# A streaming encoder step on one core: small matmuls of the mixers given out at every second step, squares of the first sub-layer taken later and added on DVE

## The chip, the cores and the metric

The kernel runs on one core of one Trainium2 chip. The metric is device time in microseconds (us) of one execution; lower is better. The kernel before has a median of 1207.81 us over three runs (1206.51 to 1208.27). Times inside an execution come from one profiled run. The engines are named as in the profile: PE (TensorE, with PEld for its weight loads), DVE (VectorE), ACT (ScalarE), POOL (GpSimd) and SP (SyncE, which issues DMAs).

## The reference

The trunk has two layers. Each layer has three sub-layers with a norm in front and a norm behind: a half-step SwiGLU, a mixer, and another SwiGLU. All of it is fp32. 304 tokens are worked on at once: 16 meta tokens, 256 prompt frames and 32 frames of a running stream. The model width is 1024, the hidden width of the SwiGLU 2816.

```python
def half_ffn(x, g_pre, w_in, w_out, g_post):
    gate, up = jnp.split(rmsnorm(x, g_pre) @ w_in, 2, axis=-1)
    return x + 0.5 * rmsnorm((jax.nn.silu(gate) * up) @ w_out, g_post)
# mixer: z = pre_mix(x) @ w_in; z -> attn q,k,v | ret q,k,v | ret gate
p = exp(s - m) / (sum(exp(s - m)) + exp(sink - m))        # chunk-banded attention with a sink
scores = einsum('bnihd,bnjhd->bnhij', rot(q), rot(k)) * intra_decay   # retention
o = scores @ v + q_decay * (rot(q) @ state)
ret = o * rsqrt(mean(o * o) + EPS) * silu(gate)           # norm over each head, then the gate
x = x + rmsnorm(concat(attn, ret) @ w_out)
```

Per layer and mixer there are 8 attention heads in 2 groups and 8 retention heads in 4 pairs. Besides the final norm's result, the kernel writes the attention caches and the retention states.

## The kernel before, in words

Activations lie transposed, features on the 128 partitions and tokens along the free axis, so a product is a matmul of a 128x128 weight block with 128x304 activations. An fp32 product is made of three matmuls of a reduced type (`mm3`): high part of the weight by high part of the activation (L257), low by high (L258), high by low (L260). These are called large matmuls here; nearly all of PE's work is of them. Weights come from DRAM as raw tiles (SP's queue, L187 and L191) and are split just ahead of use: ACT copies the high part (L205), DVE subtracts to get the low part (L208).

A `group4` keeps four PSUM banks open and works through eight weight pieces of 12 large matmuls each, a `group2` keeps two open, with 6 large matmuls between its calls of `tick`. Nothing in the program waits by itself: the order in which instructions are written is the order in each engine's queue, and `tick(ns)` sets it. It advances a clock that stands for PE's time (775 for 6 large matmuls, 1550 for 12), splits the next weights, runs the jobs in `later` that are due, and then takes jobs from two threads: "a" (attention) and "r" (retention). Of each thread it takes one due job per call, and goes on only past a job marked as free. `flush` empties everything that is left.

A mixer (`mixer`, L765) begins with a `group4` for attention k, v and the first half of q, then nine `group2` (L1197 to L1207): the second half of q, then twice retention k, q and v, then the gate in two halves. What becomes ready is queued with due times:

- Attention, per unit of two chunks (`queue_attn`, L1148): scores (L1060), softmax on DVE and ACT (L1029, L1031, L1034, then L1038 to L1046), transposes of the probabilities (L1074) copied by ACT (L1083) and DVE (L1081), and their product with v (L1092). Units of the running stream and of the meta tokens have lines 1115, 1125 and 1139 for the same steps.
- Retention, per pair of heads p (`queue_ret`, L924): transposes of v (L887), scores (L900) multiplied by the decay on DVE (L905), output (L915 to L921) copied by ACT (L922), its square on ACT (`norm_sq`, L947), the norm's matmul (L952) with square root on ACT (L954), reciprocal on DVE (L955) and multiply on POOL (L956), and transposes of k (L845). Before that, rotated q and k are made: DVE multiplies as soon as a `group2` ends (L821, L822), SP moves rows (L825), POOL adds a `ROT` later (L828).

Behind the gate's two groups comes `flush` (L1208) and `gate_out`: silu on ACT (L1179), multiply on DVE (L1180), and the split of the product into high (L1182, ACT) and low (L1184, DVE). The output projection follows: its first four pieces are attention's, the other four the retention's.

The first sub-layer of the program has no sub-layer ahead of it, so `pre_norm` puts its work into `later` (L472 to L478): `prep(k)` makes the high half of activation k on ACT (L424) and the low half on DVE (L427); `stat_sq(k)` squares on ACT (L432) and adds on POOL (L434). Two buffers, tag "sq", hold squares. After the first `group4`, `stats` sums over the partitions with a matmul of ones (L483), and a square root (L486) and a reciprocal (L491) follow.

Of the kernel before, what the change touches and what calls it, by code (L numbers as in the profile page):

```python
# [17 lines left out]
KD = DM // P  # L18
# [25 lines left out]
X2 = 1000  # L44
TAILF = 4
CAP0 = 14
SQ0 = 500
SQD = 500
PREP = 800
KA = 6  # L50
START = (11000, 11713)
# [55 lines left out]
def tile_hybrid_step(ctx, tc, I, O):  # L107
    nc = tc.nc
    PE, ACT, DVE, POOL, SP = nc.tensor, nc.scalar, nc.vector, nc.gpsimd, nc.sync
# [7 lines left out]
    def bank():  # L117
        return ps.tile([P, 512], F32, tag="bk", name="bk")
# [48 lines left out]
    xw = []  # L167
# [7 lines left out]
        xw.pop().close()  # L175

    raws, split = {}, {}
    st = {"dma": 0, "split": 0, "use": 0, "free": 0, "xw": None, "cap": 1 << 30, "ramp": 0}

    def load_to(c, between=lambda: None):  # L180
        while st["dma"] < min(c, len(chunks)):
# [13 lines left out]
    def split_one():  # L195
        i = st["split"]
        eng = ACT if i else DVE
        load_to(i // 2 + 1)
        r = raws[i // 2][:, (i % 2) * 512:(i % 2) * 512 + 512]
        if i in extra:  # L200
            hi, lo = (st["xw"].tile([P, 512], F32R, name=f"{nm}{(i - 132) % 8}") for nm in ("xhi", "xlo"))
        else:
            hi, lo = (wp.tile([P, 512], F32R, tag=nm, bufs=BUFS, name=nm) for nm in ("hi", "lo"))
        if eng is ACT:
            ACT.activation(out=hi, in_=r, func=ACTF.Copy)  # L205
        else:
            eng.tensor_copy(hi, r)
        DVE.tensor_tensor(out=lo, in0=r, in1=hi.bitcast(F32), op=ALU.subtract)  # L208
        split[i] = (hi, lo)
        if i % 2:  # L210
            raws.pop(i // 2)
        st["split"] += 1
        load_to((i + 1) // 2 + RAWS)

    def advance(most=2):
        while most and st["split"] < min(st["cap"], 2 * len(chunks)) and ring[st["split"] + 1] - ring[st["free"]] <= AHEAD and (
                st["split"] not in extra or st["xw"]):
            split_one()
            most -= 1
# [9 lines left out]
    clock = [0.0]  # L229
    later = []  # L230
    A, R = threads["a"], threads["r"]

    def tick(ns):
        clock[0] += ns
        advance()
        while later and later[0][0] <= clock[0]:
            later.pop(0)[1]()
        for nm, q in threads.items():
            while q and clock[0] >= q[0][1]:
                f, _, free = q.pop(0)  # L240
                f()
                if not free:
                    break
# [18 lines left out]
    def group4(nk, xh, xl, n, order, done, tail=2, lead=1):  # L262
        bk = [bank() for _ in range(4)]
        ws = [piece() for _ in range(lead)]
        for part in range(2):
            for k in range(lead):
                for m in range(4):
                    mm3(bk[m][:, :n], ws[k], m, xh(k), xl(k), k == 0, False, (part,))
                st["free"] += part
                if lead > 1 or part:  # L270
                    tick(1550 if lead == 1 else 1033 - 516 * part)
        for k in range(lead, nk - tail):
            w = piece()
            for m in range(4):
                mm3(bk[m][:, :n], w, m, xh(k), xl(k), False, False)
            st["free"] += 1
            tick(1550)
        ws = [piece() for _ in range(tail)]
        st["last"] = ws[-1][0], xh(nk - 1), n
        for i, m in enumerate(order):  # L280
            for j in range(tail):
                k = nk - tail + j
                mm3(bk[m][:, :n], ws[j], m, xh(k), xl(k), k == 0, k == nk - 1)
            done(m, bk)
            if i == 3:
                st["free"] += tail
            tick(388 * tail)
        return bk
# [59 lines left out]
    def x_in(hf, w=(0, 0, 0)):  # L348
        for t, (t0, tn) in enumerate(TT):
            b = xb[3 * hf + t]  # L350
            if (hf, t) == (0, 2):
                PE.transpose(out=b[:, 64:80], in_=gr, identity=ident[0:16, 0:16])
            for k in range(4):
                PE.transpose(out=b[:, k * P:k * P + tn], in_=xtok[t][0:tn, (4 * hf + k) * P:(4 * hf + k + 1) * P],
                             identity=ident[0:tn, 0:tn])
            warm(w[t])
            src = b.rearrange("p (k t) -> p k t", k=4)[:, :, 0:tn]
            dst = x[:, 4 * hf:4 * hf + 4, t0:t0 + tn]
            if t == 1:
                ACT.activation(out=dst, in_=src, func=ACTF.Copy)  # L360
            else:
                if (hf, t) == (0, 2):
                    DVE.tensor_copy(gcol[:, 0:16], b[:, 64:80])
                DVE.tensor_copy(dst, src)
# [55 lines left out]
    def acts(n, dt=F32R):  # L420
        return [ap.tile([P, N], dt, tag="act", bufs=2 * KD, name="act") for _ in range(n)]

    def act_hi(k, ua, pre):
        ACT.activation(out=ua[k][:, T0:], in_=x[:, k, T0:], func=ACTF.Copy, scale=gain(*pre, k))  # L424

    def act_lo(k, ua, pre):
        DVE.scalar_tensor_tensor(out=ua[KD + k][:, T0:], in0=x[:, k, T0:], scalar=gain(*pre, k),  # L427
                                 in1=ua[k][:, T0:].bitcast(F32), op0=ALU.mult, op1=ALU.subtract)

    def stat_sq(k, acc, first, eng=POOL):  # L430
        sq = acc if k == first else ap.tile([P, N], F32, tag="sq", bufs=2, name="sq")
        ACT.activation(out=sq[:, T0:], in_=x[:, k, T0:], func=ACTF.Square)  # L432
        if k != first:
            eng.tensor_tensor(out=acc[:, T0:], in0=acc[:, T0:], in1=sq[:, T0:], op=ALU.add)  # L434

    def small(name, tag=None, bufs=1):
        return ap.tile([P, N], F32, tag=tag or name, bufs=bufs, name=name)

    def pre_norm(pre, prev):

        ua = acts(2 * KD)
        acc = small("acc")
        rb = small("rb")
        if prev:
            lo0 = prev.first(ua)
            for k in range(1, KD + 1):
                if k < KD:
                    prev.step(k)
                    act_hi(k, ua, pre)
                if k == 1:  # L450
                    lo0()
                if k > 2:
                    act_lo(k - 1, ua, pre)
                if k < 2:
                    act_lo(k, ua, pre)
                if k > 1:
                    stat_sq(k - 1, acc, 1, DVE if k > KA else POOL)
            prev.residual0()
            stat_sq(0, acc, 1, DVE)
        else:  # L460
            for k in range(4):
                act_hi(k, ua, pre)
                split_one()
                act_lo(k, ua, pre)

            def rest():
                x_in(1)
                start.close()

            def prep(k):  # L470
                act_hi(k, ua, pre)
                act_lo(k, ua, pre)  # L472
            later.append((X2, rest))
            for k in range(4, KD):
                later.append((X2 + PREP * (k - 3), lambda k=k: prep(k)))
            for k in range(KD):
                later.append((X2 + SQ0 + SQD * k, lambda k=k: stat_sq(k, acc, 0)))
            later.sort(key=lambda e: e[0])  # L478
        st["cap"] = st["use"] + (11 if prev else CAP0)

        def stats():
            b = bank()
            PE.matmul(out=b[:, T0:N], lhsT=ones, rhs=acc[:, T0:], start=True, stop=True)  # L483
            sd = small("sd")
            if prev is None:
                ACT.activation(out=sd[:, T0:], in_=b[:, T0:N], func=ACTF.Sqrt, scale=1.0 / DM, bias=epst)  # L486
            else:
                DVE.scalar_tensor_tensor(out=sd[:, T0:], in0=b[:, T0:N], scalar=1.0 / DM, in1=prev.se[:, T0:], op0=ALU.mult,
                                         op1=ALU.add)
                ACT.activation(out=sd[:, T0:], in_=sd[:, T0:], func=ACTF.Sqrt)  # L490
            DVE.reciprocal(out=rb[:, T0:], in_=sd[:, T0:])  # L491
            st["cap"] = 1 << 30

        return (lambda k: ua[k][:, T0:]), (lambda k: ua[KD + k][:, T0:]), rb, stats
# [85 lines left out]
    def ffn(pre, post, nxt, prev, after=None):  # L580
        last = nxt is None
        xh, xl, rb, stats = pre_norm(pre, prev)
        if after:
            after()
# [180 lines left out]
    def mixer(l, prev):  # L765
        nonlocal T0
        lastl = l == DEPTH - 1
        t0 = NMETA if lastl else 0
        xh, xl, rb, stats = pre_norm((2, l), prev)
        mix = ExitStack()  # L770
        mp = mix.enter_context(tc.tile_pool(name="mix", bufs=1, reuse_waits="tile"))
# [490 lines left out]
```

## Time and profile before

| what | kernel before |
|---|---|
| median of three runs | 1207.81 us (1206.51 to 1208.27) |
| profiled execution: its own time | 1207.66 us |
| profiled execution: span of the trace | 1205.9 us |
| mean granted clock of PE | 0.994 of full |
| PE busy, instructions | 1181.7 us, 8746 |
| DVE busy, instructions | 833.0 us, 1503 |
| ACT busy, instructions | 589.6 us, 1208 |
| POOL busy, instructions | 184.2 us, 198 |

Busy time is the time in which an engine had an instruction of its own running; overlapping matmuls count once. The page of the profile gives it for the span, and again in 40 slices. For a kernel that is bound by one engine, the share says little on what a change is worth; the timeline (each instruction with its start and length), the waits (what an engine stood still for) and the chain of waits (followed back from the last instruction) say more. In the timeline, neighbours of one form on one engine are folded into one row with a count (x2), whose length is from the start of the first to the end of the last. Two engines' rows are interleaved by start. A bracket at the end gives the idle time of the engine just before and what ended it.

### The profile page before, as it was taken

What the parts mean: (1) busy time and instruction counts of PE and PEld (TensorE: products, weight loads), DVE (VectorE), ACT (ScalarE), POOL (GpSimd) and SP (SyncE); (2) the same over time, 40 slices, a digit from 0 to 9 for tenths busy, and PEclk for the clock granted to TensorE, in tenths of its full rate; (3) what the DMA queues carried; (4) which work ended last, traced back from release to release, by engine and by line L of the source; (5) the groups of instructions that cost most, each with busy time, mean ns of one, the idle gap of its engine ahead of it and who ended that gap; (6) DMA issues with size and microseconds to landing.
All of it is one profiled execution on the core that took longest, in us unless ns stands there. A gap on an engine that the chain in (4) does not pass through costs nothing. (4 is left out here: it accounts for less than half of the span.)

```text
span 1205.9 us, 22846 instructions
## 1 busy us (share of the span) xinstructions
PE 1181.7 (98%) x8746; PEld 1147.7 (95%) x8746; DVE 833.0 (69%) x1503; ACT 589.6 (49%) x1208; POOL 184.2 (15%) x198
## 2 busy tenths in 40 slices
PE   8999999999999999999999999999999999999996
PEld 8999999998899999999989999999988999999996
DVE  6766664587888766675586665747778988666543
ACT  6644444455455545444454444445554655454441
POOL 4200001130143200022030000313101353000000
PEclk9999999999999999999999999999999999999998
DMA  7655455633425554544616445556434436645531
GB/s 227 175 170 177 142 177 158 206 120 109 125 73 156 159 174 141 174 157 158 207 56 192 141 155 172 176 155 202 127 91 133 127 97 191 203 141 170 189 113 40
DMA packets 155917, 182.64 MB, mean 151 GB/s; under 512 B 12144, under 2 KB 126368, under 8 KB 155552
## 3 DMA queue, kind: packets, MB, share of 16 engines
q1 hardware_dynamic: 153760, 178.51, 48.1%
q0 software_dynamic: 1344, 1.76, 0.7%
q8 instruction: 68, 1.11, 0.4%
q10 hardware_dynamic: 704, 0.93, 0.2%
q14 instruction: 41, 0.34, 0.1%
HBM read 175.83 MB, written 2.23 MB: 148 GB/s over the span
## 5 line engine op out<-in xcount | busy, mean ns | idle before, releaser
L257 PE MATMUL bk<-act,hi 128*128 128x304 f32 (+1 forms) x1696 | 515.8, 306 | 2.2 <-ACT hi L205 1.8
L208 DVE TENSOR_TENSOR lo<-raw,hi 128x512 fp32r<-128x512 f32 x616 | 420.7, 729 | 126.5 <-ACT hi L205 123.4
L258 PE MATMUL bk<-act,lo 128*128 128x304 f32 (+1 forms) x1696 | 506.1, 300 | 0.7 <-DVE lo L208 0.6
L260 PE MATMUL bk<-act,hi 128*128 128x304 f32 (+1 forms) x1696 | 490.4, 301 | 2.7 <-DVE act L427 1.3
L205 ACT ACTIVATE hi<-raw 128x512 fp32r<-128x512 f32 x615 | 351.6, 622 | 136.4 <-PE bk L260 111.6
L257 PEld LDWEIGHTS bk<-act,hi 128*128 128x128 f32 x1696 | 319.7, 188 | 8.4 <-issue 3.4
L258 PEld LDWEIGHTS bk<-act,lo 128*128 128x128 f32 x1696 | 319.8, 189 | 2.0 <-DVE lo L208 1.3
L260 PEld LDWEIGHTS bk<-act,hi 128*128 128x128 f32 x1696 | 313.5, 189 | 4.2 <-DVE act L1184 2.4
L257 PE MATMUL bk<-hh,hi 128*128 128x304 f32 (+1 forms) x704 | 210.7, 300 | 0.0
L258 PE MATMUL bk<-hh,lo 128*128 128x304 f32 (+1 forms) x704 | 210.3, 299 | 0.0
L260 PE MATMUL bk<-hl,hi 128*128 128x304 f32 (+1 forms) x704 | 207.8, 301 | 0.0
L595 ACT ACTIVATE sg<-tg 128x304 f32<-128x304 f32 (+1 forms) x88 | 40.0, 455 | 197.6 <-DVE tg L594 197.6
L257 PEld LDWEIGHTS bk<-hh,hi 128*128 128x128 f32 x704 | 132.5, 188 | 0.4 <-issue 0.2
L258 PEld LDWEIGHTS bk<-hh,lo 128*128 128x128 f32 x704 | 132.3, 188 | 0.0
L260 PEld LDWEIGHTS bk<-hl,hi 128*128 128x128 f32 x704 | 131.0, 188 | 0.0
L594 DVE TENSOR_TENSOR tg<-bk,rb 128x304 f32<-128x304 f32 (+1 forms) x88 | 41.0, 466 | 87.2 <-PE bk L260 87.1
L574 POOL TENSOR_TENSOR x<-x,rs 128x304 f32<-128x304 f32 (+1 forms) x40 | 45.4, 1168 | 292.3 <-DVE rs L570 292.3
L599 DVE TENSOR_TENSOR hl<-tu,hh 128x304 fp32r<-128x304 f32 (+1 forms) x88 | 41.5, 471 | 46.9 <-ACT hh L598 45.6
L598 ACT ACTIVATE hh<-tu 128x304 fp32r<-128x304 f32 (+1 forms) x88 | 40.0, 455 | 60.5 <-DVE tu L597 60.5
L513 POOL TENSOR_TENSOR acc<-acc,sq 128x304 f32<-128x304 f32 (+1 forms) x12 | 10.0, 837 | 323.7 <-ACT sq L510 323.0
L546 POOL TENSOR_TENSOR x<-x,s 128x304 f32<-128x304 f32 (+1 forms) x35 | 31.3, 930 | 141.7 <-ACT s L538 141.7
L597 DVE TENSOR_TENSOR tu<-tu,sg 128x304 f32<-128x304 f32 (+1 forms) x88 | 42.7, 486 | 14.1 <-ACT sg L595 9.4
(255 smaller groups left out, 1071.5 us busy)
## 6 DMA issues: line engine op xcount, KB each, us to landing
raw<-in_ffn_w_in_dram SPq DMA_DIRECT2D x352, 256.0 KB, 4.6
raw<-in_ffn_w_out_dram SPq DMA_DIRECT2D x88, 512.0 KB, 4.8
raw<-in_w_in_dram SPq DMA_DIRECT2D x36, 512.0 KB, 4.2
raw<-in_w_out_dram SPq DMA_DIRECT2D x16, 512.0 KB, 4.0
raw<-in_w_in_dram SPq DMA_DIRECT2D x16, 256.0 KB, 3.0
dec<-in_dec_dram SPq DMA_DIRECT2D x2, 1280.0 KB, 7.0
t<-t SPq DMA_DIRECT2D x24, 76.0 KB, 2.1
t<-t SPq DMA_DIRECT2D x8, 72.0 KB, 2.1
```

Of the source, the lines that this page charges most:

```text
L205: ACT.activation(out=hi, in_=r, func=ACTF.Copy)
L208: DVE.tensor_tensor(out=lo, in0=r, in1=hi.bitcast(F32), op=ALU.subtract)
L257: PE.matmul(out=out, lhsT=a, rhs=xh, start=first, stop=False)
L258: PE.matmul(out=out, lhsT=b, rhs=xh, start=False, stop=False)
L260: PE.matmul(out=out, lhsT=a, rhs=xl, start=False, stop=last)
L546: POOL.tensor_tensor(out=x[:, j, T0:], in0=x[:, j, T0:], in1=self.s[:, T0:], op=ALU.mult)
L574: POOL.tensor_tensor(out=x[:, k, T0:], in0=x[:, k, T0:], in1=self.rs[:, T0:], op=ALU.mult)
L594: DVE.tensor_tensor(out=tg[:, T0:], in0=bk[j][:, :n], in1=rb[:, T0:], op=ALU.mult)
L595: ACT.activation(out=sg[:, T0:], in_=tg[:, T0:], func=ACTF.Silu)
L597: DVE.tensor_tensor(out=tu[:, T0:], in0=tu[:, T0:], in1=sg[:, T0:], op=ALU.mult)
L598: ACT.activation(out=hh[a][:, T0:], in_=tu[:, T0:], func=ACTF.Copy)
L599: DVE.tensor_tensor(out=hl[a][:, T0:], in0=tu[:, T0:], in1=hh[a][:, T0:].bitcast(F32), op=ALU.subtract)
```

## The change

The change has two parts. Jobs of the two threads are given out only when the clock has gone on by at least 1500 since the last time: in a `group2`, whose steps are 775 long, that is at every second step, 12 large matmuls apart. `later` and the splitting of weights stay at every step. And in the first sub-layer the squares fall due from 6000 on and 850 apart instead of from 1500 on and 500 apart; seven are added on DVE and the last one on POOL. (One of the eight starts the sum and isn't added: six adds move to DVE and one stays on POOL.)

```diff
@@ -44,8 +44,9 @@
 X2 = 1000
 TAILF = 4
 CAP0 = 14
-SQ0 = 500
-SQD = 500
+SQ0 = 6000
+SQD = 850
+QUANT = 1500
 PREP = 800
 KA = 6
 START = (11000, 11713)
@@ -175,7 +176,7 @@
         xw.pop().close()
 
     raws, split = {}, {}
-    st = {"dma": 0, "split": 0, "use": 0, "free": 0, "xw": None, "cap": 1 << 30, "ramp": 0}
+    st = {"dma": 0, "split": 0, "use": 0, "free": 0, "xw": None, "cap": 1 << 30, "ran": 0}
 
     def load_to(c, between=lambda: None):
         while st["dma"] < min(c, len(chunks)):
@@ -235,6 +236,9 @@
         advance()
         while later and later[0][0] <= clock[0]:
             later.pop(0)[1]()
+        if clock[0] - st["ran"] < QUANT:
+            return
+        st["ran"] = clock[0]
         for nm, q in threads.items():
             while q and clock[0] >= q[0][1]:
                 f, _, free = q.pop(0)
@@ -474,7 +478,7 @@
             for k in range(4, KD):
                 later.append((X2 + PREP * (k - 3), lambda k=k: prep(k)))
             for k in range(KD):
-                later.append((X2 + SQ0 + SQD * k, lambda k=k: stat_sq(k, acc, 0)))
+                later.append((SQ0 + SQD * k, lambda k=k: stat_sq(k, acc, 0, DVE if k < KD - 1 else POOL)))
             later.sort(key=lambda e: e[0])
         st["cap"] = st["use"] + (11 if prev else CAP0)
```

In the new file the lines from 49 on stand one later, those from about 240 on four later: L432 is L436, L1029 is L1033.

**ACT, first sub-layer.** L432 and L436 are the squares, L205 and L206 the weight splits, L424 and L428 the high halves of the activations. Before (one more square follows behind the last row):

```order
L432 ACTIVATE acc<-x 128x304
L205 ACTIVATE hi<-raw 128x512 x2
L424 ACTIVATE act<-x,gcol 128x304
L432 ACTIVATE sq<-x 128x304 x2
L424 ACTIVATE act<-x,gcol 128x304
L432 ACTIVATE sq<-x 128x304
L205 ACTIVATE hi<-raw 128x512 x2
L424 ACTIVATE act<-x,gcol 128x304
L432 ACTIVATE sq<-x 128x304 x2
L424 ACTIVATE act<-x,gcol 128x304
L432 ACTIVATE sq<-x 128x304
L205 ACTIVATE hi<-raw 128x512 x2
```

After:

```order
L206 ACTIVATE hi<-raw 128x512 x2
L428 ACTIVATE act<-x,gcol 128x304 x2
L206 ACTIVATE hi<-raw 128x512 x2
L428 ACTIVATE act<-x,gcol 128x304 x2
L206 ACTIVATE hi<-raw 128x512 x2
L436 ACTIVATE acc<-x 128x304
L206 ACTIVATE hi<-raw 128x512
L436 ACTIVATE sq<-x 128x304 x2
L206 ACTIVATE hi<-raw 128x512
L436 ACTIVATE sq<-x 128x304 x5
L490 ACT_TABLE_LOAD
```

The squares stood between the high halves, and now stand behind all of them, the last five in a row ahead of the square root of the sum (L490).

**DVE, first mixer, where a retention q group ends.** L1029 and L1031 (L1033 and L1035 after) open the softmax of one attention unit, L821 and L822 (L825 and L826) are the rotation's multiplies at the end of a retention q group, L208 (L209) is a weight split, L1081 (L1085) copies transposed probabilities of the unit before. Before:

```order
L208 TENSOR_TENSOR lo<-raw,hi 128x512
L1029 COPY bk<-nsinkp 128x2
L1031 TENSOR_REDUCE sm<-bk 128x1 x2
L1029 COPY bk<-nsinkp 128x2
L1031 TENSOR_REDUCE sm<-bk 128x1 x2
L821 TENSOR_TENSOR t_3474<-bk,cr 128x304
L822 TENSOR_TENSOR t_3473<-bk,cr 128x304
L821 TENSOR_TENSOR t_3474<-bk,cr 128x304
L822 TENSOR_TENSOR t_3473<-bk,cr 128x304
L208 TENSOR_TENSOR lo<-raw,hi 128x512
L1081 COPY pT<-bk 64x256
```

After:

```order
L209 TENSOR_TENSOR lo<-raw,hi 128x512
L825 TENSOR_TENSOR t_3456<-bk,cr 128x304
L826 TENSOR_TENSOR t_3455<-bk,cr 128x304
L825 TENSOR_TENSOR t_3456<-bk,cr 128x304
L826 TENSOR_TENSOR t_3455<-bk,cr 128x304
L209 TENSOR_TENSOR lo<-raw,hi 128x512
L1033 COPY bk<-nsinkp 128x2
L1035 TENSOR_REDUCE sm<-bk 128x1 x2
L1033 COPY bk<-nsinkp 128x2
L1035 TENSOR_REDUCE sm<-bk 128x1 x2
L209 TENSOR_TENSOR lo<-raw,hi 128x512
L1085 COPY pT<-bk 64x256
```

The softmax's first steps stood ahead of the rotation and now stand behind it and behind one split, and a split more stands ahead of the copy.

**ACT, end of the first mixer.** L922 (L926) copies the output of a retention pair, L947 (L951) squares it, L954 (L958) is the root behind the norm's matmul, L1179 (L1183) the gate's silu, here its table. Before:

```order
L922 ACTIVATE osb<-bk 128x304
L205 ACTIVATE hi<-raw 128x512
L947 ACTIVATE sq<-osb 128x304
L922 ACTIVATE osb<-bk 128x304
L205 ACTIVATE hi<-raw 128x512
L954 ACTIVATE gsd<-bk,epst 128x304
L947 ACTIVATE sq<-osb 128x304
L205 ACTIVATE hi<-raw 128x512
L954 ACTIVATE gsd<-bk,epst 128x304
L205 ACTIVATE hi<-raw 128x512
L1179 ACT_TABLE_LOAD
```

After:

```order
L926 ACTIVATE osb<-bk 128x304
L206 ACTIVATE hi<-raw 128x512
L951 ACTIVATE sq<-osb 128x304
L926 ACTIVATE osb<-bk 128x304
L958 ACTIVATE gsd<-bk,epst 128x304
L951 ACTIVATE sq<-osb 128x304
L958 ACTIVATE gsd<-bk,epst 128x304
L1183 ACT_TABLE_LOAD
```

A weight split stood ahead of each of the two roots; now none does, and the third pair's root and the fourth's square and root follow one another directly ahead of the gate.

## Rows read from the trace of the kernel before

**Rows 1.** The page's first part: busy time, share and instructions by engine.

```profile
PE 1181.7 (98%) x8746; PEld 1147.7 (95%) x8746; DVE 833.0 (69%) x1503; ACT 589.6 (49%) x1208; POOL 184.2 (15%) x198
```

**Rows 2.** Timeline of DVE and POOL, first sub-layer: start and length in us, engine.

```profile
12.36 0.53 DVE L427 SCALAR_TENSOR_TENSOR act<-x,gcol,act 128x304 fp32r<-128x304 f32 x1
...
17.13 2.17 DVE L427 SCALAR_TENSOR_TENSOR act<-x,gcol,act 128x304 fp32r<-128x304 f32 x2
...
21.75 2.14 DVE L427 SCALAR_TENSOR_TENSOR act<-x,gcol,act 128x304 fp32r<-128x304 f32 x2
...
17.09 2.93 POOL L434 TENSOR_TENSOR acc<-acc,sq 128x304 f32<-128x304 f32 x3 [14.60 <-ACT sq L432]
```

**Rows 3.** Timeline of PE, end of the program's first group.

```profile
21.43 0.30 PE L260 MATMUL bk<-act,hi 128*128 128x304 f32 x1
21.57 0.30 PE L257 MATMUL bk<-act,hi 128*128 128x304 f32 x1
...
22.90 0.40 PE L260 MATMUL bk<-act,hi 128*128 128x304 f32 x1 [0.90 <-DVE act L427]
...
26.69 0.67 PE L483 MATMUL bk<-acc,ones 128*128 128x304 f32 x2
```

**Rows 4.** Groups by line: count, busy us, mean ns, idle before and releaser.

```profile
L434 DVE TENSOR_TENSOR acc<-acc,sq 128x304 f32<-128x304 f32 (+1 forms) x15 | 7.7, 513 | 2.9 <-ACT sq L432 2.9
```

**Rows 5.** Timeline, first mixer: the first attention unit behind its softmax.

```profile
278.05 0.15 DVE L1029 COPY bk<-nsinkp 128x2 f32<-128x2 f32 x1
...
279.18 0.46 DVE L821 TENSOR_TENSOR t<-bk,cr 128x304 f32<-128x304 f32 x1
...
280.67 0.65 ACT L1083 ACTIVATE pT<-bk 80x256 f32<-80x256 f32 x2
...
281.43 0.41 DVE L1081 COPY pT<-bk 64x256 f32<-64x256 f32 x1
...
281.89 0.43 PE L1092 MATMUL bk<-pT,vpF 64*64 64x128 f32 x4
```

**Rows 6.** Waits of the weight load, first mixer, then second: total us, times, longest.

```profile
PEld bk L1092 <- ACT pT L1083: 0.7, 2, 0.4
PEld bk L900 <- POOL qr L828: 0.5, 1, 0.5
...
PEld bk L1092 <- ACT pT L1083: 1.2, 2, 0.6
PEld bk L952 <- ACT sq L947: 0.5, 1, 0.5
```

**Rows 7.** Timeline of PE, first mixer: retention scores between large matmuls.

```profile
331.41 0.30 PE L260 MATMUL bk<-act,hi 128*128 128x304 f32 x1
331.64 1.13 PE L900 MATMUL bk<-qr,kr 64*128 64x272 f32 x12
332.70 0.41 PE L257 MATMUL bk<-act,hi 128*128 128x304 f32 x1
332.95 0.30 PE L258 MATMUL bk<-act,lo 128*128 128x304 f32 x1
```

**Rows 8.** Timeline, end of the first mixer: norms, gate, output projection.

```profile
342.23 0.68 PE L952 MATMUL bk<-sq,blk 128*128 128x304 f32 x2
343.00 0.51 ACT L954 ACTIVATE gsd<-bk,epst 128x304 f32<-128x304 f32 x1 [0.66 <-PE bk L952]
343.41 0.45 ACT L947 ACTIVATE sq<-osb 128x304 f32<-128x304 f32 x1
343.55 2.05 DVE L955 RECIPROCAL gsd<-gsd 128x304 f32<-128x304 f32 x1 [0.48 <-ACT gsd L954]
...
350.04 3.18 DVE L1180 TENSOR_TENSOR osb<-osb,zg 128x304 f32<-128x304 f32 x3
...
354.30 0.41 PE L260 MATMUL bk<-act,hi 128*128 128x304 f32 x1 [0.59 <-DVE act L1184]
```

**Rows 9.** Chain of waits, second layer's last sub-layer: start and length in us, what.

```profile
998.51 0.24 PE bk L260
```

## The prediction

> **What bounds the kernel now.** I read the page first, then the starts of the matmuls, then who waited for whom. The reader is to see that TensorE (PE) is the bound: it is called busy for 98% of the span [rows 1]. A busy PE is one with a matmul in it, so I go by starts instead: a large matmul (128x304, lines 257, 258, 260) starts 0.14 us after the one before it (21.43 to 21.57 [rows 3]). Whatever spaces two starts further is a wait or a small matmul of the mixers. So a change is worth what it adds to or takes from those spaces. DVE, ACT and POOL count only where PE waits for them, and that is at three kinds of places: the end of the first group of the first sub-layer [rows 3], some small groups of the mixers [rows 5, 6], and the start of each mixer's output projection [rows 8].
>
> The profiled execution took 1207.66 us, 1.76 of it outside the span; I sum against it. It lies 0.15 under the median of the three runs, 1207.81, and I let that go.
>
> **The squares of the first sub-layer.** No instruction goes: eight squares on ACT and seven adds stay, six adds move from POOL to DVE and all come later. Before, POOL adds from 17.09 on [rows 2], and two of DVE's subtracting multiplies (L427, which make the low halves of the activations) take 2.17 us and again 2.14, where one took 0.53 while POOL was idle [rows 2]. PE needs them: its matmul at 22.90 idled 0.90 for L427 [rows 3]. From 21.57 to the statistics matmul (L483) at 26.69 are 24 large matmuls, 24 x 0.14 = 3.36 of 5.12 us [rows 3]; 1.8 us are waits. With no add on POOL and no square on ACT ahead of them, the last L427 is done at about 20.5 (from 17.13: four of 0.53, four or so DVE splits between), and PE wants it after 23: those 1.8 us go.
>
> What is late next is the sum of squares itself. PE would reach L483 at 26.69 - 1.8 = 24.9. ACT now starts squaring behind all its other work, at about 20.0, and only two buffers hold squares, so from the third on square and add take turns: an add on DVE is 0.51 [rows 4], a square 0.45 (the same form as L947 [rows 8]). Followed step by step, the sixth DVE add ends near 25.3, POOL's last near 26.3. L483 starts at 26.35 and PE waits 1.45 there. Net -0.35. Bounds: -1.8 if the sum is in time; +0.5 if every hand-over costs 0.1 more. I take the step-by-step value.
>
> **The small matmuls, first attention unit that comes back from its softmax.** The order of PE changes: small groups now stand 12 large matmuls apart, where 6 or 18 stood between them. The first transposes (L1074) move back by 12, their consumer (L1092) only by 6. Between them ACT and DVE copy the transposed tile (L1083, L1081), and in both queues the softmax of the next unit is ahead of these copies. Before, DVE began that softmax (L1029) at 278.05, ACT reached L1083 at 280.67, and the half of L1092 that needs L1081 started at 281.89 [rows 5]. Now the four rotation multiplies and a split stand ahead of L1029, and they take 281.43 - 279.18 = 2.25 us [rows 5]. The whole chain L1029, exponentials, L1083 moves by that; a further split, which waits for ACT, stands before L1081 and adds about 0.1. So the half of L1092 comes at 281.89 + 2.3 = 284.2. PE, 6 large matmuls later than before and without its present wait of 0.3 (0.7 in two groups, the longest 0.4 [rows 6]), is there at 281.89 - 0.3 + 0.84 = 282.4. It waits 1.8 instead of 0.3: +1.5 in the first mixer. The second mixer has the same order; I take the same. Sum +3.0. Bounds: from -0.9, both present waits gone, to +6.0, twice the shift.
>
> **Waits that go.** The other consumers get more distance. The second L1092 group waits 0.4 in the first mixer and 1.2 - 0.6 = 0.6 in the second [rows 6]; as PE was held up before, the copies are in time. The L900 group of the second half waits 0.5 for POOL's rotated q in the first mixer [rows 6]; DVE's rotation now stands ahead of two reciprocals of 2 us each, as the one in [rows 8], and POOL's rotation add ahead of two norm multiplies, so this wait goes. Of 0.5 on the weight load some 0.2 is the usual start of such a group (331.41 to 331.64 [rows 7]): 0.3, and 0.3 for the second mixer alike. The wait of 0.5 for L947 in the second mixer [rows 6] goes because scores and norm are 12 matmuls further apart. Sum -2.1; bounds -2.1 and 0.
>
> **Fewer changes between large and small.** A small group of its own costs its edges: from the last large matmul to its start 0.23 instead of 0.14, and the first large one behind it holds 0.25 instead of 0.14 (332.70 to 332.95) [rows 7], together 0.20. Two groups in one place pay that once. Each mixer has three such pairs of half-array groups where it had one: 4 x 0.20 = -0.8. Pairs with transposes I take as -0.1 in all. Bounds: 0 and -2, were every removed place (some ten a mixer) worth 0.1.
>
> **The end of each mixer.** This is the cost that the diff hides. The give-outs come too late for the last two norms, so they fall into the flush ahead of the gate. PE now meets, without a large matmul between: the last retention output (L921), the norm matmul of the third pair (L952), that of the fourth. The fourth waits for a chain on ACT: L954 of the third, 0.77 after its L952 (342.23 to 343.00), then the square L947 0.41 later, which takes 0.45 [rows 8]. With a hand-over that is 1.7 from the end of L921, and PE would have been there after 0.5: a wait of 1.2 us. Behind it the gate: DVE does both reciprocals in a row, about 2.0 apart; the third pair's begins 0.77 + 0.55 = 1.3 after L921 ends (343.00 to 343.55 is the 0.55), so the first gate multiply (L1180) starts 1.3 + 2 x 2.0 = 5.3 after it; from L1180 to the matmul that needs the first low half it is 350.04 to 354.30, 4.26 [rows 8]: 9.5. PE is at that matmul 1.7 + 0.6 + 49 x 0.14 = 9.15 after (0.6 for the last L952 and the change to large ones, 49 for the four attention steps and the first of the fifth). It waits 0.4 there, where it waited 0.75 (idle 0.59 and a slow start [rows 8]). So +1.2 - 0.4 = +0.8 a mixer, +1.6. Bounds: +0.4 and +5.
>
> **Sum.** -0.35 + 3.0 - 2.1 - 0.9 + 1.6 = +1.2, which gives 1207.66 + 1.2 = 1208.9 us. A measurement of this kernel tells a difference of about 0.2%, 2.4 us, from none; this is none.
>
> **Rivals.** First, faster: DVE gets through the rotation before PE arrives, so the first L1092 groups wait no longer than now. For it: DVE has idle stretches ahead of many of its steps. Against: the rotation reads a bank that PE closes just before it. It gives 1208.9 - 3.0 = 1205.9, and with the sum of squares in time too 1204.4.
>
> Second, slower: the end of each mixer is a serial chain of norm, reciprocal, gate and split, and all of it comes to lie on PE's path. It decides if the first L1180 starts over 7 us after the last L921, for example because POOL's norm multiply slows DVE there as it does with L427. Each mixer then pays 1.7 us more than in my sum: 1212.3. Against: four attention steps of the projection, 6.7 us of PE work, cover it.
>
> Third, slower: the new waits cost the clock. Near 998.51, behind a wait for weights, 14 large matmuls start 0.24 apart, not 0.14 [rows 9]: 14 x 0.10 = 1.4 us. Four new waits with such a stretch each give 1208.9 + 5.6 = 1214.5. Against: behind the waits before 22.90 and 354.30 [rows 3, 8] matmuls start 0.14 apart from the second one on. The Trainium skill ("TensorE: Matmul & The Clock Gate", What's actually happening) says that the clock is granted for sustained activity and withdrawn in idleness; this rule would give the third rival's time. The trace agrees for the long wait near 998.51, and not for the short ones.
>
> Fourth, the thinning does nothing that PE feels, waits only change places: the first sub-layer alone counts, 1207.3.
>
> **How the numbers follow.** The forecast 0.45, its own range 1206.3 to 1211.3; first rival 0.22, second 0.18, third 0.05, fourth 0.10. Below 1205.4 lie most of the first rival and a little of the forecast: faster 0.18. Above 1210.2 lie the second and third and the upper edge of the forecast: slower 0.29. The same: 0.53. The range 1203.4 to 1213.3 reaches to the first and second rivals' times and 1 us beyond, since runs of the kernel before alone lie from 1206.51 to 1208.27.
>
> **What would show it.** In the profile after: L427 at 0.53 each in the first 21 us, and L483 preceded by a wait of 1 to 2 us; the first L1092 group of each mixer with a wait of about 1.8 us, the second with none; L900 without a wait for POOL; the last L952 of each mixer idle for about 1.2 us; the wait for L1184 shorter. I am wrong if the first L1092 groups do not wait longer, if the last L952 does not wait, or if a small group that is fine now waits for over 1 us.

## The result and the profile after

The changed kernel has a median of 1217.29 us over four runs (1215.72 to 1218.5); the kernel before, run beside it, 1207.16. The ratio is 1.0085 with a 95% interval of 1.0073 to 1.0097: 10 us slower. The forecast was 1208.9 us within 1203.4 to 1213.3. The profiled span went from 1205.9 to 1216.7 us, while PE's busy time hardly rose ([rows 1] have 1181.7):

```profile
PE 1185.1 (97%) x8746; PEld 1151.9 (95%) x8746; DVE 831.2 (68%) x1509; ACT 589.7 (48%) x1208; POOL 178.4 (15%) x192
```

Both kernels start the same 7776 large matmuls in the same sequence, so counting them gives cuts that fall on the same work in every trace. The time between such cuts (us, from the starts in one profiled execution of each; the four right columns are experiments, below):

| stretch | before | changed | thinning from first unit on | wait filled, 12 | rotation behind | late copy in before |
|---|---|---|---|---|---|---|
| first group and statistics | 20.32 | 20.77 | 20.43 | 20.40 | 21.10 | 20.91 |
| first mixer with its projection | 111.92 | 116.96 | 111.73 | 114.83 | 114.27 | 116.09 |
| second mixer with its projection | 107.09 | 111.42 | 106.55 | 108.18 | 108.32 | 112.72 |
| behind it, 16 us | 15.97 | 16.56 | 16.77 | 16.06 | 16.82 | 16.08 |
| next 30 us | 29.93 | 30.84 | 31.16 | 30.13 | 29.99 | 28.56 |

The rest agrees within 0.1. Of the 10.8 us between the spans, 5.0 and 4.3 came in the mixers, 0.5 in the first group (it also began 0.5 earlier), and 1.5 behind the second mixer.

In the mixers one place stands out. In the timeline of the changed kernel's first mixer (answering to [rows 5]; start and length in us):

```profile
275.91 0.15 DVE L1033 COPY bk<-nsinkp 128x2 f32<-128x2 f32 x1
...
278.35 1.16 ACT L206 ACTIVATE hi<-raw 128x512 fp32r<-128x512 f32 x2
...
279.03 0.69 DVE L209 TENSOR_TENSOR lo<-raw,hi 128x512 fp32r<-128x512 f32 x1 [1.70 <-ACT hi L206]
279.64 0.47 DVE L825 TENSOR_TENSOR t<-bk,cr 128x304 f32<-128x304 f32 x1
...
281.58 0.30 PE L264 MATMUL bk<-act,hi 128*128 128x304 f32 x1
...
281.76 0.15 DVE L1033 COPY bk<-nsinkp 128x2 f32<-128x2 f32 x1
...
284.38 0.64 ACT L1087 ACTIVATE pT<-bk 80x256 f32<-80x256 f32 x2
...
284.80 1.12 PE L1096 MATMUL bk<-pT,vpE 80*64 80x128 f32 x8 [2.93 <-ACT pT L1087]
...
286.48 0.62 PE L261 MATMUL bk<-act,hi 128*128 128x304 f32 x1
286.90 0.46 PE L262 MATMUL bk<-act,lo 128*128 128x304 f32 x1
...
289.43 0.46 PE L264 MATMUL bk<-act,hi 128*128 128x304 f32 x1
289.82 1.65 PE L1064 MATMUL bk<-kd,qa 64*128 64x192 f32 x8
```

The same places before, beyond those in [rows 5]:

```profile
274.32 0.15 DVE L1029 COPY bk<-nsinkp 128x2 f32<-128x2 f32 x1
...
280.74 0.30 PE L260 MATMUL bk<-act,hi 128*128 128x304 f32 x1
...
282.26 0.41 PE L257 MATMUL bk<-act,hi 128*128 128x304 f32 x1
```

L1033 at 281.76 opens the third unit's softmax, which began at 278.05 before; the copy L1087 comes as much later, 3.7 us; PE stands 2.93 us. And then large matmuls take 0.46 and start 0.254 apart, and the scores 1.65 us (0.92 before). The view by stretches (from and to, length, busy us of PE, PEld, DVE, ACT and POOL with instructions, granted clock, share of the DMA engines, GB/s) has the clock at full ahead of the wait and at half behind it, 1.2 of the two levels 1.2 and 2.4 GHz.

```profile
262.00:281.00 19.00, 19.00 (x145) 17.89 (x144) 13.83 (x38) 8.55 (x32) 3.76 (x5) 1.00 0.59 170
...
284.80:290.00 5.20, 5.20 (x26) 4.23 (x28) 4.43 (x11) 2.88 (x8) 1.47 (x1) 0.50 0.62 181
```

From the large matmul before this group to the one behind it the changed kernel takes 3.4 us more than before (281.58 to 286.48 against 280.74 to 282.26), the eleven starts behind it cost 11 x 0.115 = 1.3, the scores 0.9: 5.6 us at one place, of which 2.9 are the longer wait and 2.7 the slower clock. The rest of the mixer is 0.5 shorter. In the second mixer the same sum is 5.8, 3.2 of it wait, and the rest is 1.4 shorter. The waits of the weight load, first mixer, then second (answering to [rows 6]: total, times, longest):

```profile
PEld bk L1096 <- ACT pT L1087: 3.2, 1, 3.2
...
PEld bk L956 <- ACT sq L951: 0.8, 1, 0.8
...
PEld bk L1096 <- ACT pT L1087: 3.9, 1, 3.9
...
PEld bk L956 <- ACT sq L951: 1.4, 1, 1.4
```

The second L1092 wait and the wait for POOL are gone. The end of the first mixer, against [rows 8]:

```profile
350.48 0.78 PE L956 MATMUL bk<-sq,blk 128*128 128x304 f32 x2
352.27 0.78 PE L956 MATMUL bk<-sq,blk 128*128 128x304 f32 x2 [1.01 <-ACT sq L951]
...
351.90 3.97 DVE L959 RECIPROCAL gsd<-gsd 128x304 f32<-128x304 f32 x2 [1.33 <-ACT gsd L958]
355.78 2.48 DVE L1184 TENSOR_TENSOR osb<-osb,zg 128x304 f32<-128x304 f32 x3
```

PE waits 1.01 us for the fourth square; the two reciprocals follow one another, and no wait for the first low half (L1188) is left. The first sub-layer, against [rows 2, 3]:

```profile
16.95 0.97 DVE L431 SCALAR_TENSOR_TENSOR act<-x,gcol,act 128x304 fp32r<-128x304 f32 x2
...
23.82 1.61 ACT L436 ACTIVATE sq<-x 128x304 f32<-128x304 f32 x3 [0.53 <-DVE acc L438]
...
26.55 0.78 PE L487 MATMUL bk<-acc,ones 128*128 128x304 f32 x2 [2.00 <-POOL acc L438]
```

Two low halves take 0.97 where they took 2.17, PE has no wait for L431 left, and stands 2.00 us at the statistics matmul instead.

### The profile page after: what moved, and what is told of

Same layout as the page of the kernel before. It is cut to its first block, busy times and chain, and to the rows that moved or that the text cites. A ratio compares the mean times of both kernels' runs of the same rounds, so it can differ in the third digit from the quotient of the medians.

```text
span 1216.7 us, 22850 instructions
## 1 busy us (share of the span) xinstructions
PE 1185.1 (97%) x8746; PEld 1151.9 (95%) x8746; DVE 831.2 (68%) x1509; ACT 589.7 (48%) x1208; POOL 178.4 (15%) x192
## 5 line engine op out<-in xcount | busy, mean ns | idle before, releaser
L209 DVE TENSOR_TENSOR lo<-raw,hi 128x512 fp32r<-128x512 f32 x616 | 420.2, 727 | 133.2 <-ACT hi L206 130.2
L206 ACT ACTIVATE hi<-raw 128x512 fp32r<-128x512 f32 x615 | 351.7, 622 | 136.8 <-PE bk L264 107.5
L603 DVE TENSOR_TENSOR hl<-tu,hh 128x304 fp32r<-128x304 f32 (+1 forms) x88 | 41.5, 471 | 48.8 <-ACT hh L602 45.0
```

What stands on the lines that cost most here:

```text
L603: DVE.tensor_tensor(out=hl[a][:, T0:], in0=tu[:, T0:], in1=hh[a][:, T0:].bitcast(F32), op=ALU.subtract)
```

## The experiments

Ratios are to runs of the kernel before on the same chip, with a 95% interval. Theory A: the loss is the wait at the first unit's product with v, and the clock behind it. Lines of code left out of a cut are marked with `...`.

**The two parts apart.** Thinning alone keeps the old squares (`SQ0 = SQD = 500`, POOL); squares alone has `QUANT = 0`.

> Theory A: nearly all of the 10.1 us comes from the thinning, and in each mixer from one place: the first attention unit's product with v (L1096) stands 2.9 us for ACT's copy L1087, and the clock stays at its lower level for about 4.9 us behind that wait. The squares count for nothing (their trace shows the old waits of 1.6 us gone and a new one of 2.3 us at the statistics matmul). So thinning alone gives 1217 +- 1 us, 10 over the kernel before. Rival B: the squares cost part of it themselves; then this kernel lies 1 us or more under 1217.

> Theory A: the change in the squares alone is worth nothing that can be measured: 1207.6 us, at most 0.6 from the kernel before on either side, with the L427 waits gone and a wait of about 2.3 us before the statistics matmul (two stretches that cancel to +0.45). Rival B: it costs 1 us or more.

Thinning alone 1216.88 us (1.0084, 1.0071 to 1.0097); squares alone 1207.72 (1.0004, 0.9995 to 1.0013). So the loss is the thinning's.

**The other phase.**

```diff
+        st["ran"] -= 775
         group2(*xq, N - t0, done_q(1))
```

> The same thinning and the same squares, but the small matmuls are given out at the first, third, fifth and seventh step of each two-bank group instead of the second, fourth, sixth and eighth. The softmax of the third attention unit then stands ahead of the rotation on DVE. Theory A: the copy L1087 comes some 4.6 us after the third unit's scores, PE arrives 4.7 us after them, so the wait of 2.9 us shrinks to 0.3 or so, and with it the clock's stretch goes: 5.2 us less in each mixer, 1207 us in all (1205.5 to 1208.5). Rival D: giving out in twos loses time at many places, a little each, since every chain is stretched; then the phase doesn't matter much, and this stays above 1213 us.

1214.29 us (1.006, 1.0048 to 1.0073): 3 us back, not 10. The wait shrank to 1.62 only. The timeline's row of PE, and that of the run with the rotation behind, told of further down:

```profile
284.06 0.71 PE L1096 MATMUL bk<-pT,vpE 80*64 80x128 f32 x8 [1.62 <-ACT pT L1087]
```
```profile
283.75 0.71 PE L1102 MATMUL bk<-pT,vpE 80*64 80x128 f32 x8 [1.43 <-ACT pT L1093]
```

My expectation counted from the third unit's scores. But the copy stands on ACT behind the exponentials of the second unit, a weight split, and those of the third; this phase puts the second unit's scores 36 large matmuls ahead of L1096 instead of 48. From the second unit's first exponential to the copy is 5.5 us in this run and before, 7.6 in the changed kernel, where the rotation lies between.

**The wait filled.** The 20 or 12 matmuls on constants give nothing to the output.

```diff
+FILL = 20          # then 12
...
             def pv():
-                ob = bank()[:, 0:4 * CH].rearrange("p (j c t) -> p j c t", j=2, c=2)
+                ob = bank()
+                if g == 0 and c0 == 1:
+                    for _ in range(FILL):
+                        PE.matmul(out=ob[:, 0:P], lhsT=ident, rhs=ones, start=True, stop=True)
+                ob = ob[:, 0:4 * CH].rearrange("p (j c t) -> p j c t", j=2, c=2)
```

> The changed kernel with 20 additional matmuls of 128 columns on constants in each mixer, right ahead of the first unit's L1096 products, into the bank that these overwrite; some 2.8 us of PE work in a wait of 2.9 us. Theory A: the wait itself stays (L1096 starts at the same time), but the clock doesn't fall, so the 12 products, the 12 large matmuls and the scores behind them run at the full clock: 2.9 us less in each mixer, 1217.3 - 5.8 = 1211.5 us. Rival E: the slower stretch behind the wait has another cause than PE standing still (its operands or the banks); then nothing is gained, 1217 us or more.

1214.05 us (1.0056, 1.0043 to 1.0068). The 20 took 4.63 us and held PE beyond the copies; the clock stayed at 1.00. So 12:

> As the run that fills the wait, with 12 matmuls on constants instead of 20. The 20 took 4.63 us, not 2.8, and held PE beyond the copies by some 1.8 us. 12 take 2.8 us, no longer than the wait. Theory A: 1.8 us less in each mixer than with 20, the clock still full behind the wait: 1214.05 - 3.6 = 1210.5 us. So the slower clock alone is worth 1217.1 - 1210.5 = 6 to 7 us of the loss. Rival G: the full clock of that run came from the long stretch of constants, and 2.8 us of them behind a large group isn't enough in the second mixer, where the wait is 3.6: 1213 us.

1211.82 us (1.0035, 1.0022 to 1.0047). Timeline and stretch:

```profile
282.06 2.84 PE L1095 MATMUL bk<-ones,c_ident 128*128 128x128 f32 x24
...
285.71 0.71 PE L1101 MATMUL bk<-pT,vpE 80*64 80x128 f32 x8 [0.81 <-ACT pT L1088]
...
284.00:290.00 6.00, 5.11 (x44) 4.03 (x43) 3.89 (x10) 4.12 (x16) 1.48 (x1) 1.00 0.51 132
```

From the start of the last large matmul ahead to the products it is 3.78 us in the first mixer and 3.50 in the second, against 3.22 and 3.92 in the changed kernel: in sum they come no earlier. Yet 5.5 us of the loss are gone, 2.1 and 3.2 in the two mixers by the traces. So the slower clock is about half of the loss, and PE's standing still brings it. The forecast was 1.3 too low.

**The rotation behind the softmax.**

```diff
-                if m == 1:
+                if m == 1 and i == 0 and dst is qr:
+                    def turn(t=clock[0] + ROT):
+                        later.append((t, rotate(bk, i, dst)))
...
+                    later.append((clock[0] + 1000, turn))
...
+                elif m == 1:
```

> The changed kernel, but in each mixer the DVE multiplies of the first half's q rotation (L825, L826) are written one step later, behind the third attention unit's first softmax steps. Theory A2 (A, mended by the last runs: the chain to the copy L1087 hangs on the second unit's softmax, behind it on ACT's splits, and on the rotation): two splits now stand ahead of L1033 and end at about 280.2 where L1033 began at 281.76, so the chain is 1.5 us earlier and the wait is 1.4 instead of 2.9. A wait of 1.6 in the other phase still brought the slower clock, so a part of that loss may stay: 1214.3 with all of it, 1208.5 with none. Rival F: the rotation is not what delays the copy (ACT's own queue does); then nothing moves, 1217 us.

1211.29 us (1.0038, 1.0023 to 1.0054), between its two ends. The wait is 1.43, as worked out (row above); the granted clock in the 5.35 us behind it is 0.69.

**The thinning elsewhere.** From the first unit's L1096 on only; then also ended ahead of the gate's groups; then with the squares due earlier.

```diff
-        if clock[0] - st["ran"] < QUANT:
+        if clock[0] - st["ran"] < st["quant"]:     # 0 at the start
...
             def pv():
+                if g == 0 and c0 == 1:
+                    st["quant"] = QUANT
...
+        st["quant"] = 0                            # ahead of each mixer
         first = group4(KD, xh, xl, N, (2, 3, 0, 1), lambda m, bk: stats() if m == 0 else None, lead=2)
...
+        st["quant"] = 0                            # second and third kernel only
         group2(xh, xl, n, done_g(0))
```

> The squares as changed; the thinning begins in each mixer only behind the first unit's products with v (L1096 of the changed kernel), so that the order up to there is that of before. Theory A2: that one place is the whole loss and the rest of the thinning gains 0.5 to 1 us a mixer through fewer changes between large and small groups: 1207.5 - 1.5 = 1206.0 us (1205 to 1207.5). Rival D (a little is lost at many places): 1210 us or more.

1209.34 us (1.002, 1.0011 to 1.0028). Its waits in the first mixer:

```profile
PEld bk L956 <- ACT sq L951: 2.3, 2, 1.5
...
PEld bk L1098 <- ACT pT L1087: 0.6, 2, 0.3
```

The first unit's wait is back at 0.3. With the old order up to there the mixers take 0.2 and 0.5 us less than before (table): the place is all of the mixers' loss. But the median is 2.6 us more, and in the trace 2.0 us more lie in the two stretches behind the second mixer.

> As the run that thins behind the first unit, and the thinning also ends ahead of the gate's two groups, so that the last two norms are given out before the flush as in the kernel before. That run was 2.6 us over the kernel before although its two mixers were 0.2 and 0.5 us shorter; behind its second mixer 0.8 us are lost at the statistics matmul (964 to 980 us) and more at a wait for weights near 1000. Theory T (tail): with both reciprocals in the flush the gate's chain on DVE and ACT ends later, the weight splits behind it too, the raw tiles come free 1 us later and the next sub-layer's loads start 1 us later. Then this kernel has the 16.0 us between 964 and 980 again and is at 1207 us (1206 to 1208). Rival H: the loss behind the second mixer does not hang on the tail; then 1209 us.

1208.55 us (1.0011, 1.0002 to 1.002): between the two.

> The same with the squares due from 4500 on and 600 apart. By theory T 1206.5 us, at or a little under the kernel before, and the best that the two parts of the change give together; by rival H 1208.5 us.

1207.65 us (1.0003, 0.9994 to 1.0012).

> The changed kernel with the thinning switched off in the gate's two groups only. The first unit's wait and its slow stretch stay. Theory T: the loss behind the second mixer goes, 0.6 us at the statistics matmul and up to 1 us near 1000: 1217.1 - 1.3 = 1215.8 us. Rival H: 1217 us.

1216.49 us (1.0074, 1.006 to 1.0087). These three do not tell theory T from H by time. By traces the statistics' stretch is 16.33, 16.29 and 16.05 us, partly back; the next 30 us are 31.44, 30.91 and 30.09. What differs there is seen in the waits (changed kernel, then tail undone):

```profile
POOL qr L878 <- DMA kr<-qr: 5.1, 1, 5.1
...
PE bk L261 <- ACT hi L206: 2.6, 1, 2.6
DVE hl L603 <- POOL qr L878: 2.5, 1, 2.5
```
```profile
POOL qr L878 <- DMA kr<-qr: 3.2, 1, 3.2
...
PE bk L261 <- ACT hi L206: 1.6, 1, 1.6
```

Four DMAs exchange rows of the retention state on SP's queue, and POOL adds the exchanged rows (L878). In nine of fourteen traces, the kernel before's among them, their packets take 2.33 to 2.35 us; in five (the changed kernel, thinning alone, and the runs from the first unit on, in the middle, and in the middle with squares) 3.3 to 3.9. In those five, a 16 KB packet of the instruction queue starts 1.8 to 2.1 us after the exchange begins and lasts 0.9 to 1.5; in the others it starts at 2.28 or later, or none falls into it. And in those five the exchange's last two packets start only where that packet ends, within 0.02 us. The rest of the path is in the waits: POOL's add comes later by as much, DVE's L603 stands 2.2 to 2.5 us for it, ACT's part of the SwiGLU follows, and behind that, without a wait of its own, stands the weight split for which PE waits, 2.6 to 3.0 us instead of 1.6. This is seen in all fourteen traces and not tried by an experiment; nor is it settled why the 0.6 us at the statistics come and go.

**The squares earlier.**

```diff
-SQ0 = 6000
-SQD = 850
-QUANT = 1500
+SQ0 = 4500
+SQD = 600
+QUANT = 0
```

> No thinning; squares on DVE as changed, but due from 4500 on and 600 apart instead of 6000 and 850. Reading of the squares' run: the old waits of PE for L427 (1.6 us) are gone, and the new one at the statistics matmul (2.3 us) is there since the last five squares come in a row at the end. Given out earlier, the sum is in time: 2.0 us less at the statistics matmul and at most 0.5 more for the low halves: 1207.5 - 1.5 = 1206.0 us. Rival: the squares ahead of the low halves bring the old waits back, 1207.5 us.

1206.25 us (0.9995, 0.9987 to 1.0004): no change, and the wait at the statistics matmul is still 2.02. ACT began the squares at 19.21 instead of 19.79 only, since high halves and splits lie ahead in its queue, and from the third on square and add take turns over two buffers. The trace bears out neither the expected gain nor the rival's old waits.

**The reverse.** The kernel before, with one copy made nine times:

```diff
-                            ACT.activation(out=pT[0:n, u, i], in_=src, func=ACTF.Copy)
+                            for _ in range(9 if g == 0 and c0 == 1 and u == 0 else 1):
+                                ACT.activation(out=pT[0:n, u, i], in_=src, func=ACTF.Copy)
```

> The kernel before, with ACT's first copy of the first unit's transposed probabilities (L1083) made nine times instead of once in each mixer; eight more at some 0.32 us put the copy 2.6 us later and nothing else of the order changes. Theory A: PE stands some 2.6 us longer at this one place and then loses another 2.7 us to the slower clock behind it: 5.3 us a mixer, 1207 + 10.6 = 1217.5 us, as slow as the changed kernel. Rival I: a wait costs its own length and no more (the slow stretch of the changed kernel has to do with its thinner order): 1212 us.

1216.53 us (1.0077, 1.0064 to 1.0089), 9.1 over the kernel before. Timeline and stretch:

```profile
284.77 0.71 PE L1093 MATMUL bk<-pT,vpE 80*64 80x128 f32 x8 [3.36 <-ACT pT L1084]
...
286.18 0.46 PE L258 MATMUL bk<-act,lo 128*128 128x304 f32 x1
...
286.00:289.00 3.00, 3.00 (x14) 2.42 (x14) 2.32 (x7) 2.15 (x7) 0.42 (x1) 0.50 0.19 66
```

A late copy alone, in the old order, makes the kernel nearly as slow as the change did. The added waits came out longer than planned, 3.3 and 3.4 us, and the mixers take 4.2 and 5.6 us more: 0.9 and 2.2 us beyond the waits. So rival I, with these waits, would be at 1207.4 + 6.7 = 1214.1, and the run lies 2.4 above it; theory A holds, but the clock took 3.1 us here and not the 5.4 that were expected.

No version is faster than the kernel before by more than can be measured.

## Why the prediction was wrong

**The step that failed: the first attention unit's wait.** The place and the direction were right; its price was forecast as +1.5 a mixer and measured as 5.6 and 5.8. Two things were missing.

First, the size of the wait. I moved the third unit's softmax by what now stands ahead of it, 2.25 us, and left the second unit's where it was. But that one is given out later too: its L1029 stood at 274.32 before and its L1033 at 275.91, 1.6 later. ACT's weight split (278.35) stands behind its exponentials, DVE's split (279.03) waits for ACT's, and the rotation and the third unit's softmax stand behind that. So the copy came 3.7 us later, not 2.25 (3.7 = 1.6 + 2.1), and PE stood 2.93 us, not 1.8. The run with the rotation behind gave 1.5 us of the wait back, as this chain says.

Second, the clock. I had it as the third rival, at 0.05 and with 1.4 us a wait, because matmuls behind the present waits of under 1 us start 0.14 apart. But the rows held a second case, the slow starts near 998.51 [rows 9] (the trace has eleven in a row, not 14; with the slow ones at their edges they cost the 1.4 us all the same), and the wait ahead of them is 1.6 us long; a wait of 1.8 us belonged to that case as much as to the other. The fill shows the size: the clock is some 5.4 us of the loss, both mixers together, 2.7 a wait and not 1.4. The reverse shows the same mechanism in the old order. The Trainium skill ("TensorE: Matmul & The Clock Gate", What's actually happening) has the rule that I set aside: the clock is granted for sustained activity. The traces agree here, with 0.50 behind 2.93 us of standing still.

**What was right.** Waits that go: the second L1092 groups and L900 have none. Fewer changes between large and small: 28 small groups in the first mixer where 35 were; outside the first unit's place the two mixers are 0.5 and 1.4 us shorter (forecast 1.4 over both: 2.1 and 0.9 less, 1.6 more at the ends). The end of each mixer: PE's wait for the fourth square 1.01 in the first (1.2 forecast), none for L1188 (0.4 forecast). The first sub-layer: -0.35 forecast, +0.45 by trace, nothing by time; the wait moved from the low halves to the sum, as described.

**What was not in it.** A carry-over behind the second mixer: 1.5 us in the changed kernel's trace. 0.9 of it goes with the longer wait behind the state's exchange; the 0.6 at the statistics matmul has no cause shown. The thinning's own small gain goes there.

## What to carry to other kernels

When instructions are given out at other steps, follow the late consumer's chain back through every queue to the first instruction that also moved; what newly stands ahead of one link is only part of its delay. A wait of TensorE is priced as its length only if the trace has waits of that length with the clock full behind them; here a wait of 2.9 us cost nearly as much again. Filling such a wait with idle matmuls, or delaying a copy on purpose, tells the two prices apart in one run each.

## What the hardware showed that was not expected

The same wait may or may not cost the clock. The changed kernel and the one with the tail undone have the same first sub-layer and both stand 2.0 us at the statistics matmul; behind it, the first has a granted clock of 1.00 and the second of 0.55 (stretches of PE, changed kernel, then tail undone):

```profile
27.00:31.00 4.00, 4.00 (x30) 3.90 (x29) 2.91 (x3) 2.22 (x3) 4.00 (x8) 1.00 0.28 64
```
```profile
26.87 0.78 PE L487 MATMUL bk<-acc,ones 128*128 128x304 f32 x2 [2.02 <-POOL acc L438]
...
27.30:31.00 3.70, 3.70 (x17) 3.63 (x16) 2.66 (x3) 1.90 (x3) 3.70 (x8) 0.55 0.26 55
```

That costs the second 1.5 us in this execution. Longer waits differ in their price too. From the first large matmul behind the first unit's products to the one behind the next scores it is 2.72 us with the wait filled, 4.92 in both mixers of the changed kernel, and 3.94 and 4.68 with thinning alone, whose waits are 3.04 and 3.33.

Near 1000 us a wait of 1.6 us is followed by one or two slow starts in three traces (squares alone, 20 matmuls on constants, the reverse) and by ten or more in the others with that wait. So waits of 1.4 to 2.4 us cost the clock in some places and executions and not in others, and no run here shows what decides. It may be some of the spread of 2 to 4 us between executions of one kernel.
